# A gated delta rule in chunks of 128 tokens instead of 64, inside a two-layer float32 trunk

## The chip, the cores and the metric

The kernel runs on one core of a Trainium2 chip, as one program with one launch. The metric is the device time of the whole program in microseconds (us), less is better. Five engines work side by side, each through its own instructions in order: TensorE (PE; its weight loads are shown apart as PEld), VectorE (DVE), ScalarE (ACT), GpSimd (POOL) and SyncE (SP), which here only issues DMA transfers.

## The reference

Two layers over 1024 tokens of width 1024, all in float32. Layer 0 is softmax attention over a band of chunks and an MLP; layer 1 is a gated delta rule (8 heads of 128) and an MLP; every MLP is a squared ReLU of width 4096. The change touches the delta rule alone. Per head and per chunk of tokens the reference does this:

```python
gc = jnp.cumsum(g, axis=-1)                      # log decay within a chunk
decay = jnp.exp(jnp.where(incl, gc[..., :, None] - gc[..., None, :], -jnp.inf))
L = jnp.where(strict, jnp.einsum('bhnid,bhnjd->bhnij', kb, k) * decay, 0.0)
M = L + jnp.eye(CHUNK)
sol = lax.linalg.triangular_solve(M, rhs, lower=True, unit_diagonal=True)  # gives u and w
qk = jnp.einsum('bhnid,bhnjd->bhnij', q, k) * decay
def step(state, inp):                            # one chunk after the other
    v_new = u_c - w_c @ state
    o_c = qd_c @ state + qk_c @ v_new
    state = state * gl_c + kd_c.T @ v_new
```

CHUNK is 64 in the reference. The result of the recurrence does not depend on the chunk's length; a longer chunk means fewer steps of `step` and a larger triangular system.

## The kernel before

The program is one stream: attention, its output projection and MLP (lines 569 to 1640), the delta rule (`deltanet`, lines 1674 to 2582), then the second output projection and MLP. Activations are stored transposed, 128 features by 1024 tokens.

The delta rule's stage is planned while the program is written out. `dn_run` walks through 34 dense panels (w_in for k, q, v and z of 8 heads, then two panels of the output projection, named "o"), each of 128 output features; a panel is two halves of 24 matmuls of 128x512 (the two "o" panels here are one half each). After every dense matmul `turn()` lets each of some ten tasks emit a step if a cost table (`Clock`) says that its inputs are ready and its engines are not too far behind; tasks are asked in the order of `PRIORITY`. What comes out is a fixed order on each engine. So the small work of the delta rule stands between the dense matmuls on PE, and a wait of a small matmul holds up the dense matmuls behind it. Where the dense matmuls need something that is not there by the table, `idle()` moves the table's time on.

The tasks, all per head of 8 pairs of 64-token chunks (128 tokens a pair, index p):

- `dn_decays`: adds a mask to the log decays (POOL), takes exp (ACT, one instruction per pair), writes to DRAM the two 64x64 blocks on the diagonal of each 128x128 square.
- `dn_blocks`: k times k on PE, times the decays on DVE (tile U); writes U's 32x32 diagonal blocks (`ud`) and the 32x32 block beside them in each 64 (`u12`) to DRAM.
- `dn_solves`: inverts the 32x32 triangular blocks of four heads at once on DVE (tiles fz, ft, fu).
- `dn_inverse`: builds the inverse of each 64x64 triangle from the 32x32 ones: read `u12` back, scale by rk (POOL), 16 matmuls of 32x32 (`tp<-xa,ua`), scale on DVE, 16 more (`tp<-Zh,ua`), copy into Z on ACT.
- `dn_prep_keys`, `dn_prep_queries`, `dn_prep_values`: transposes, q times k with the decays read back (tile dc, scaled by rk on POOL), the products with Z that give u (tile vb) and w (half of tile WQ; the other half is q times its decay, written by POOL).
- `dn_scans(odd)`: the recurrence, one task for even heads and one for odd ones. Per chunk of 64: one matmul of the state st with 128 columns of WQ, which hold w of this chunk and the decayed q of the same chunk side by side (`s<-st,WQ`), then DVE forms vn, then `s<-vn,kd` and `s<-vn,qk` on PE, then DVE forms the next state st and ACT copies 64 rows of the output (o). kd and qk are full 128x128 operands, whose other half meets zeros in vn or qk.
- `dn_outs`, `dn_reload`: norm and gate of a head's output, transposes (`tp<-ident,o`), to DRAM and back as the two-part operands xs of the output projection.

Names of tiles in the trace leave buffer numbers out: s is both PSUM tiles of the scan (s1 and s2), tp the shared auxiliary PSUM bank (two buffers), acc the dense one. A float32 matmul of 128x128 leaves two records in the trace, a dense one (float32r) leaves one. Nearly all instructions of the stage have line 163, that of the helper which records them, so groups are told apart by tiles.

Of the kernel before, what the change touches and what calls it, by code (L numbers as in the profile page):

```python
# [7 lines left out]
F32 = mybir.dt.float32  # L8
# [199 lines left out]
class Trunk:  # L208
# [1465 lines left out]
    def deltanet(self, rhs, finish):  # L1674

        tc = self.tc
        with ExitStack() as es:
# [10 lines left out]
                "s1": Ring(2, lambda: self.sc.tile([P, P], F32, name=self.nm("s1"), tag="s1")),  # L1688
# [186 lines left out]
    def dn_gates(self):  # L1875
# [12 lines left out]
        self.u12 = self.dr.tile([8, 2, 32, 8, 32], F32, name="u12")  # L1888
        d1.tile([P, 16], F32, name="room3")
# [6 lines left out]
        self.vn = [[d1.tile([P, P], F32, name=f"vn{o}{e}") for e in range(2)] for o in range(2)]  # L1896
        for v in self.vn:
            for e in range(2):
                nc.gpsimd.memset(v[e][64 - 64 * e : 128 - 64 * e], 0.0)

        self.qks = [d1.tile([P, 8, P], F32, name=f"qk{n}") for n in range(2)]
        for qk in self.qks:
            for e in range(2):
                nc.gpsimd.memset(qk[64 * e : 64 * e + 64, :, 64 * e : 64 * e + 64], 0.0)
# [18 lines left out]
        nc.gpsimd.memset(mask[0:64, 64:128], -BIG)  # L1923
# [23 lines left out]
        for s in (1, 2, 4, 8, 16, 32):  # L1947
            va, vb = (t.rearrange("q (e t) -> q e t", e=2) for t in (g0, g1))
            nc.vector.tensor_copy(vb[:, :, :s], va[:, :, :s])
            nc.vector.tensor_tensor(vb[:, :, s:], va[:, :, s:], va[:, :, : 64 - s], ALU.add)  # L1950
            g0, g1 = g1, g0
        gc = g0
        gv = gc.rearrange("q (e t) -> q e t", e=2)
        eg, ed, bg, ng, nb = t64("eg"), t64("ed"), t64("bg"), t64("ng"), t64("nb")
        nc.scalar.activation(eg, gc, AF.Exp)
        nc.vector.tensor_tensor(
            ed.rearrange("q (e t) -> q e t", e=2), gv[:, :, 63:64].broadcast_to([NQ, 2, 64]), gv, ALU.subtract)
# [8 lines left out]
        for n, t in enumerate((gc, nb, eg)):  # L1966
# [62 lines left out]
    def dn_decays(self, odd):  # L2029
# [3 lines left out]
        for h in range(odd, 8, 2):  # L2033
# [127 lines left out]
    def dn_blocks(self):  # L2161

        nc, db = self.nc, self.db
        for h in range(8):
# [88 lines left out]
    def dn_inverse(self, h):  # L2253
# [3 lines left out]
        X = self.dq.tile([P, 8, 32], F32, name=self.nm("xa"), tag="xa")  # L2257
        U12 = self.dq.tile([P, 8, 32], F32, name=self.nm("ua"), tag="ua")
        for e in range(2):
# [11 lines left out]
        for b in range(4):  # L2271
# [3 lines left out]
            if b % 2 == 0:  # L2275
                nc.sync.dma_start(X[s], xd[r].rearrange("p c i -> c p i"))
# [23 lines left out]
        yield  # L2300
        for e in range(2):
            r, o = slice(64 * e, 64 * e + 32), slice(64 * e + 32, 64 * e + 64)
            nc.scalar.activation(Z[r, :, o], ps[r], AF.Copy)
        self.give("tp", tp)
# [50 lines left out]
    def dn_prep_queries(self):  # L2355
        nc, db = self.nc, self.db
        for h in range(8):
            yield from self.until("q", h)
            qT = self.heads.pop(("q", h))
            dc = self.dq.tile([P, HB], F32, name=self.nm("dc"), tag="dc").rearrange("p (q t) -> p q t", t=64)  # L2360
# [310 lines left out]
```

## Time and profile before

| | |
|---|---|
| runs | 2565.44, 2566.76, 2565.82 us; median 2565.82 |
| profiled execution | 2565.74 us, of which the span from first to last instruction is 2564.0 |
| PE, PEld busy | 96%, 80% of the span |
| DVE, ACT, POOL busy | 72%, 47%, 50% |
| mean granted TensorE clock | 0.990 |
| the delta rule's stage | from about 1199 us to 1838 us of the span |

A row of the chain or the timeline gives start and length in us, the engine, the line, the operation, and in brackets how long the engine was idle just before and what released it. Matmuls are pipelined, so what one costs is read from the distance between starts, not from the length of a record. A group's row (by line, operation and tile) has the count, the busy time in us and the mean of one in ns, then the idle time before its instructions. A row of a window gives its borders, its length, each engine's busy time, the granted clock, the DMA share and GB/s.

### The profile page before, as it was taken

How to read it: one execution, taken by the hardware profiler on the slowest of the kernel's cores; microseconds unless marked ns; L12 is line 12 of the kernel's file. 1: busy time of each engine (PE TensorE's matmuls, PEld its weight loads, DVE VectorE, ACT ScalarE, POOL GpSimd, SP SyncE). 2: the span in 40 equal slices, each digit the busy share in tenths (PEclk: the TensorE clock that was granted, in tenths of full speed). 3: DMA queues.
4: the chain of work that ended last, by engine and by line, in shares of the span. 5: the costliest groups of instructions: out<-in, count | busy, mean ns of one | idle time of the engine just before them, and what ended most of it. 6: DMA issues, size and time to landing. Idle time of an engine off the chain costs nothing.

```text
span 2564.0 us, 36694 instructions
## 1 busy us (share of the span) xinstructions
PE 2462.7 (96%) x12638; PEld 2055.4 (80%) x12638; DVE 1848.5 (72%) x3299; ACT 1206.2 (47%) x2267; POOL 1280.2 (50%) x1088
## 2 busy tenths in 40 slices
PE   8999999999999999998888899999999999999997
PEld 6888888787888888886677788888787888787886
DVE  6666656678776688877588867666678777688887
ACT  6666567535555433334674333333335555433323
POOL 2444455615666466565474333332313766466655
PEclk9999999999999999999999999999999999999998
DMA  4222224424555966743443212213323555977752
GB/s 159 71 64 72 74 78 126 151 83 160 208 208 217 350 236 231 262 148 110 117 141 112 69 59 68 70 62 103 121 99 140 208 203 209 334 244 255 247 172 82
DMA packets 193082, 392.43 MB, mean 153 GB/s; under 512 B 54960, under 2 KB 61552, under 8 KB 192896
## 3 DMA queue, kind: packets, MB, share of 16 engines
q1 hardware_dynamic: 176048, 355.46, 41.2%
q10 hardware_dynamic: 16848, 34.63, 3.6%
q8 instruction: 100, 1.64, 0.3%
q14 instruction: 86, 0.70, 0.1%
HBM read 254.06 MB, written 127.57 MB: 149 GB/s over the span
## 4 chain that ended last, share of the span: by engine, by line
PE 63%; DVE 10%; issue 3%; DMA 3%; ACT 1%; POOL 1%; SPq 0%; ACTq 0%; DVEq 0%; POOLq 0%
PE y L1013 25%; PE z L1013 12%; PE acc L163 8%; PE acc L1013 7%; PE tp L163 3%; PE s L163 3%; PE acc L279 2%; PE acc L278 2%; PE acc L277 2%; DVE fz L163 1%; DVE ft L163 1%; DVE x L1518 1%; DMA xs<-gt 1%; DMA wraw<-in_w_down_dram 0%; DVE xs L394 0%
## 5 line engine op out<-in xcount | busy, mean ns | idle before, releaser
L163 PE MATMUL acc<-xs,whi 128*128 128x512 f32 x1808 | 637.9, 414 | 8.9 <-DVE xp L163 4.1
L163 PEld LDWEIGHTS acc<-xs,whi 128*128 128x128 f32 x1808 | 332.7, 191 | 58.4 <-DVE xp L163 4.9
L163 PE MATMUL acc<-xs,wlo 128*128 128x512 f32 x896 | 367.4, 410 | 3.4 <-POOL wlo L163 3.4
L1013 PE MATMUL y<-xs,whi 128*128 128x512 f32 x1008 | 311.6, 390 | 5.2 <-DVE x L1518 1.8
L163 POOL TENSOR_TENSOR wlo<-wraw,whi 128x512 fp32r<-128x512 f32 x126 | 166.8, 1324 | 253.2 <-ACT whi L163 213.3
L1028 POOL TENSOR_TENSOR s<-wraw 128x256 f32<-128x256 f32 (+1 forms) x93 | 91.7, 987 | 351.1 <-DVE a L1019 171.5
L1019 DVE TENSOR_TENSOR wlo<-wraw,whi 128x512 fp32r<-128x512 f32 (+1 forms) x182 | 209.9, 1153 | 26.3 <-ACT whi L1022 26.3
L1013 PEld LDWEIGHTS y<-xs,whi 128*128 128x128 f32 x1008 | 188.9, 188 | 47.2 <-DVE x L1518 2.6
L1022 ACT ACTIVATE whi<-wraw 128x512 fp32r<-128x512 f32 (+2 forms) x191 | 146.5, 767 | 122.9 <-PE y L1013 87.0
L1013 PE MATMUL y<-xs,wlo 128*128 128x512 f32 x504 | 196.3, 390 | 0.0
L1022 ACT ACTIVATE a<-s 128x256 fp32r<-128x256 f32 x122 | 63.8, 525 | 281.4 <-PE y L1013 143.4
L1013 PE MATMUL y<-xs,a 128*128 128x512 f32 x732 | 187.9, 392 | 7.0 <-DVE x L1518 7.0
L163 PEld LDWEIGHTS acc<-xs,wlo 128*128 128x128 f32 x896 | 171.6, 192 | 28.6 <-POOL wlo L163 5.2
L1518 DVE TENSOR_TENSOR x<-y,x 128x512 f32<-128x512 f32 x240 | 165.1, 688 | 35.0 <-PE y L1013 28.4
L1013 PEld LDWEIGHTS y<-xs,a 128*128 128x128 f32 x732 | 136.0, 188 | 40.6 <-DVE x L1518 10.9
L1013 PE MATMUL y<-xs,ahi 128*128 128x512 f32 x512 | 158.6, 391 | 7.8 <-ACT nt L1207 7.8
L1013 PE MATMUL acc<-xs,whi 128*128 128x512 f32 x528 | 162.8, 390 | 0.0
L163 POOL TENSOR_SCALAR pr<-pr,rs 128x640 f32<-128x640 f32 (+4 forms) x128 | 88.6, 696 | 128.9 <-DVE rs L163 97.8
L1013 PE MATMUL z<-xs,whi 128*128 128x512 f32 x480 | 147.8, 389 | 0.0
L1095 DVE TENSOR_TENSOR c<-c 128x512 fp32r<-128x512 f32 x112 | 120.2, 1078 | 31.2 <-POOL c L1025 28.4
L163 POOL TENSOR_TENSOR cy<-cy,cz 128x512 f32<-128x512 f32 x48 | 64.3, 1340 | 147.9 <-DVE cz L163 121.2
L163 DVE CUSTOM_DVE_ANT_0 pr<-sp,bias 128x640 f32<-128x640 f32 (+4 forms) x128 | 83.8, 655 | 63.8 <-PE sp L163 62.8
(345 smaller groups left out, 6218.7 us busy)
## 6 DMA issues: line engine op xcount, KB each, us to landing
xs<-gt SPq DMA_DIRECT2D x256, 256.0 KB, 4.7
gt<-c SPq DMA_DIRECT2D x112, 512.0 KB, 2.8
wraw<-in_w_up_dram SPq DMA_DIRECT2D x64, 512.0 KB, 3.9
wraw<-in_w_down_dram SPq DMA_DIRECT2D x64, 512.0 KB, 4.4
r<-gr SPq DMA_DIRECT2D x88, 256.0 KB, 3.5
wraw<-in_w_in_dram SPq DMA_DIRECT2D x32, 512.0 KB, 3.5
gr<-ssum ACTq DMA_DIRECT2D x62, 256.0 KB, 3.1
wraw<-in_w_qkv_dram SPq DMA_DIRECT2D x30, 512.0 KB, 3.3
```

Of the source, the lines that this page charges most:

```text
L163: return call(*args, **more)
L277: nc.tensor.matmul(ps, hi[:, k], xh, start=(k == 0), stop=False)
L278: nc.tensor.matmul(ps, hi[:, k], xl, start=False, stop=False)
L279: nc.tensor.matmul(ps, lo[:, k], xh, start=False, stop=(k == KT - 1))
L1013: nc.tensor.matmul(ps, w[:, k], x, start=bool(first and f), stop=bool(last and e), skip_group_check=True)
L1019: self.nc.vector.tensor_tensor(lo, src, hi.bitcast(F32), ALU.subtract)
L1022: self.nc.scalar.activation(hi, src, AF.Copy)
L1028: self.nc.gpsimd.tensor_tensor(out, x, y, ALU.add)
L1095: nc.vector.tensor_tensor(t[z][:, HB:].bitcast(F32R), t[z][:, HB:], t[z][:, :HB], ALU.subtract)
L1518: nc.vector.tensor_tensor(x, ps, x, ALU.add)
```

## The change

- The scan takes 8 steps of 128 tokens per head instead of 16 of 64. A step has two matmuls with the state (w and decayed q, 128 columns each) instead of one, one with kd and one with qk; vn, o and st are full 128x128. The first step of a head has no state and takes u in place of vn, without a copy. The PSUM tile s1 doubles to hold both products.
- The decays keep the whole 128x128 squares: the mask loses its cross-chunk part, one contiguous 512 KB DMA per head replaces two strided ones of 128 KB, dc doubles to 128x1024, and its scaling on POOL with it; the product of q and k with dc becomes one 128x512 DVE instruction in place of two of 64x256.
- The inverse gets a level: the 64x64 blocks of U beside the diagonal go to DRAM and back (`u34`, tile U34, named ub in the trace), are scaled by rk on POOL (64x512); 8 more 32x32 matmuls (`ua,Zh`) give the transposed corner, which ACT copies into X; 8 matmuls of 64x64 (`X,ub`), a scaling on DVE, 8 more of 64x64 (`Zh,ub`), a copy on ACT. One more block of the 32x32 inverses is loaded into X per head.
- The cumulative sum of the log decays has a seventh doubling step; memsets of vn and qk go, one of X comes.

```diff
@@ dn_decays, dn_blocks
-            for e in range(2):
-                r = slice(64 * e, 64 * e + 64)
-                nc.sync.dma_start(self.decay[h, r], v[r, :, r])
+            nc.sync.dma_start(self.decay[h], v)
...
+            nc.sync.dma_start(self.u34[h], U[0:64, :, 64:128])
@@ dn_inverse
+        nc.sync.dma_start(U34[0:64], self.u34[h])
...
+        nc.gpsimd.tensor_tensor(U34[0:64], U34[0:64], wide(self.rk[0:64, h], 64, 64), ALU.mult)
...
-            if b % 2 == 0:
-                nc.sync.dma_start(X[s], xd[r].rearrange("p c i -> c p i"))
+            if b < 3:
+                nc.sync.dma_start(self.X[s, :, 32 * (b % 2) : 32 * (b % 2) + 32], xd[r].rearrange("p c i -> c p i"))
...
+        o = slice(32, 64)
+        for p in range(8):
+            nc.tensor.matmul(ps[o, p], Z[o, p, o], hT[o, p], start=True, stop=True, tile_position=(32, 32))
+        yield
+        nc.scalar.activation(self.X[o, :, 0:32], ps[o], AF.Copy)
...
+        r, o = slice(0, 64), slice(64, 128)
+        for p in range(8):
+            nc.tensor.matmul(ps[o, p], U34[r, p], self.X[r, p], start=True, stop=True, tile_position=(0, 64))
+        yield
+        nc.vector.tensor_tensor(U34[o], ps[o], wide(nbr[o], 64, 64), ALU.mult)
...
+        for p in range(8):
+            nc.tensor.matmul(ps[r, p], U34[o, p], Z[o, p, o], start=True, stop=True, tile_position=(64, 0))
+        yield
+        nc.scalar.activation(Z[r, :, o], ps[r], AF.Copy)
@@ dn_prep_queries
-            nc.gpsimd.tensor_tensor(dc, dc, wide(self.rk[:, h], P, 64), ALU.mult)
+            nc.gpsimd.tensor_tensor(dc, dc, wide(self.rk[:, h], P, P), ALU.mult)
...
-                for e in range(2):
-                    r = slice(64 * e, 64 * e + 64)
-                    nc.vector.tensor_tensor(qk[r, s, 64 - 64 * e : P - 64 * e], ps[r, :, r], dc[r, s], ALU.mult)
+                nc.vector.tensor_tensor(qk[:, s], ps, dc[:, s], ALU.mult)
@@ dn_scans
-            for c in range(16):
...
-                    nc.tensor.matmul(ps, wq, st, start=True, stop=False, skip_group_check=True)
-                    yield
-                    nc.vector.tensor_tensor(vn[r], u[r, p], ps[r], ALU.subtract)
+            for p in range(8):
+                vn = u[:, p]
...
+                    nc.tensor.matmul(ps[:, 0], WQ[:, p, 0], st, start=True, stop=True, skip_group_check=True)
+                    ready = self.clock.end
+                    nc.tensor.matmul(ps[:, 1], WQ[:, p, 1], st, start=True, stop=False, skip_group_check=True)
+                    self.clock.end = ready
+                    yield
+                    vn = db.tile([P, P], F32, name=self.nm("vn"), tag=f"vn{odd}")
+                    nc.vector.tensor_tensor(vn, u[:, p], ps[:, 0], ALU.subtract)
...
-                nc.scalar.activation(o[r, p], ps[x], AF.Copy)
+                nc.scalar.activation(o[:, p], ps[:, 1], AF.Copy)
```

Since the order on each engine is planned, the change also moves work that its text leaves alone. Three places follow.

PE, at the inverse of head 7, while heads 5 and 6 are scanned. Before (xa and ua are the two operands of the first 32x32 products, acc the dense panel's bank):

```order
L163 MATMUL tp_16653<-xa_16215,ua_16216 32x32 x16
L163 MATMUL acc_16566<-xs_11822,whi_16393 128x512
L163 MATMUL s_3508_16672<-vn_12244,kd_16341 128x128
L163 MATMUL s_3506_16651<-vn_12244,qk_12251 128x128
L163 MATMUL acc_16566<-xs_11822,wlo_16394 128x512
L163 MATMUL s_3509_16678<-vn_12243,kd_15831 128x128
L163 MATMUL s_3503_16645<-vn_12243,qk_12250 128x128
L163 MATMUL acc_16566<-xs_11824,whi_16393 128x512
L163 MATMUL tp_16688<-Zh_12240,ua_16216 32x32 x16
L163 MATMUL acc_16566<-xs_11824,whi_16393 128x512
```

Now, at the inverse of a head late in the stage:

```order
L163 MATMUL s_3367_16192<-st_16157,WQ_15952 128x128 x2
L163 MATMUL tp_16170<-ua_15720,Zh_12239 32x32 x8
L163 MATMUL acc_16165<-xs_11810,wlo_15969 128x512
L163 MATMUL acc_16165<-xs_11812,whi_15968 128x512 x2
L163 MATMUL acc_16165<-xs_11812,wlo_15969 128x512
L163 MATMUL acc_16165<-xs_11814,whi_15968 128x512 x2
L163 MATMUL s_3371_16222<-vn_16207,kd_15497 128x128
L163 MATMUL s_3367_16192<-vn_16207,qk_12245 128x128
L163 MATMUL acc_16165<-xs_11814,wlo_15969 128x512
L163 MATMUL acc_16165<-xs_11816,whi_15968 128x512 x2
L163 MATMUL acc_16165<-xs_11816,wlo_15969 128x512
L163 MATMUL tp_16235<-X,ub_15721 64x64 x8
```

Three groups of eight small matmuls come per head, each among dense ones, and a scan step shows two matmuls with WQ.

PE, the last steps of head 7's scan, at the end of the stage. Before (acc_17974 is the first "o" panel's bank):

```order
L163 MATMUL s_3822_18071<-st_18065,WQ_17577 128x128
L163 MATMUL s_3823_18074<-vn_12245,kd_17214 128x128
L163 MATMUL s_3822_18071<-vn_12245,qk_12251 128x128
L163 MATMUL s_3825_18080<-st_18077,WQ_17577 128x128
L163 MATMUL acc_17974<-xs_17925,whi_17827 128x512 x2
L163 MATMUL acc_17974<-xs_17925,wlo_17828 128x512
L163 MATMUL s_3827_18088<-vn_12244,kd_17214 128x128
L163 MATMUL s_3825_18080<-vn_12244,qk_12251 128x128
L163 MATMUL acc_17974<-xs_17926,whi_17827 128x512
L163 MATMUL s_3830_18099<-st_18093,WQ_17577 128x128
```

Now (acc_17742 is the second half of head 7's z panel, the last one ahead of the "o" panels):

```order
L163 MATMUL s_3679_17720<-vn_17710,kd_17092 128x128
L163 MATMUL s_3674_17704<-vn_17710,qk_12246 128x128
L163 MATMUL acc_17651<-xs_11822,whi_17491 128x512 x2
L163 MATMUL acc_17651<-xs_11822,wlo_17492 128x512
L163 MATMUL s_3681_17730<-st_17724,WQ_17448 128x128 x2
L163 MATMUL acc_17651<-xs_11824,whi_17491 128x512 x2
L163 MATMUL acc_17651<-xs_11824,wlo_17492 128x512
L163 MATMUL s_3681_17730<-vn_17734,qk_12246 128x128
L163 MATMUL acc_17742<-xs_11811,whi_17491 128x512 x2
```

Before, the scan's last steps stood within the first "o" panel, two of them with no dense matmul between; now the last scan matmul stands ahead of 72 dense ones: 24 of z and 48 of the two "o" panels.

POOL, around the scaling of dc for the second head. Before:

```order
L163 TENSOR_TENSOR ua_14025<-ua_14025,rk 32x256 x2
L163 TENSOR_TENSOR wlo_14011<-wraw_13717,whi_14010 128x512
L163 TENSOR_TENSOR cy_14020<-cy_14020,cz_14021 128x512
L163 TENSOR_TENSOR dc_13905<-dc_13905,rk 128x512
L163 TENSOR_TENSOR cy_14158<-cy_14158,cz_14159 128x512
```

Now:

```order
L163 TENSOR_TENSOR cy_13919<-cy_13919,cz_13920 128x512
L163 TENSOR_TENSOR ua_13923<-ua_13923,rk 32x256 x2
L163 TENSOR_TENSOR ub_13924<-ub_13924,rk 64x512
L163 TENSOR_TENSOR dc_13902<-dc_13902,rk 128x1024
L163 TENSOR_TENSOR wlo_14045<-wraw_13727,whi_14044 128x512
```

The new scaling of ub and the longer one of dc now follow one another on POOL.

More of the change, by code (lines that the diff above doesn't have):

```diff
@@ L1687, in deltanet @@
                 "tp": Ring(2, self.aux), "acc": Ring(2, self.bank), "nt": Ring(3, self.nt),
[L1688 removed]
+                "s1": Ring(2, lambda: self.sc.tile([P, 2, P], F32, name=self.nm("s1"), tag="s1")),
                 "s2": Ring(2, lambda: self.sc.tile([P, P], F32, name=self.nm("s2"), tag="s2"))}
@@ L1888, in dn_gates @@
         self.u12 = self.dr.tile([8, 2, 32, 8, 32], F32, name="u12")
+        self.u34 = self.dr.tile([8, 64, 8, 64], F32, name="u34")
         d1.tile([P, 16], F32, name="room3")
@@ L1894, in dn_gates @@
             self.Zh.append(z)
-        self.vn = [[d1.tile([P, P], F32, name=f"vn{o}{e}") for e in range(2)] for o in range(2)]
-        for v in self.vn:
-            for e in range(2):
-                nc.gpsimd.memset(v[e][64 - 64 * e : 128 - 64 * e], 0.0)
+        self.X = d1.tile([P, 8, 64], F32, name="X")
+        nc.gpsimd.memset(self.X[0:32, :, 32:64], 0.0)
         self.qks = [d1.tile([P, 8, P], F32, name=f"qk{n}") for n in range(2)]
-        for qk in self.qks:
-            for e in range(2):
-                nc.gpsimd.memset(qk[64 * e : 64 * e + 64, :, 64 * e : 64 * e + 64], 0.0)
         yield
@@ L2303, in dn_inverse @@
             nc.scalar.activation(Z[r, :, o], ps[r], AF.Copy)
+        self.give("tp", tp)
+        yield
+        tp = yield from self.take("tp")
+        ps = tp.rearrange("p (q t) -> p q t", t=64)
+        r, o = slice(0, 64), slice(64, 128)
[3 more added lines that the diff above has]
+        nc.vector.tensor_tensor(U34[o], ps[o], wide(nbr[o], 64, 64), ALU.mult)
+        self.give("tp", tp)
+        yield
+        tp = yield from self.take("tp")
+        ps = tp.rearrange("p (q t) -> p q t", t=64)
+        for p in range(8):
+            nc.tensor.matmul(ps[r, p], U34[o, p], Z[o, p, o], start=True, stop=True, tile_position=(64, 0))
+        yield
+        nc.scalar.activation(Z[r, :, o], ps[r], AF.Copy)
         self.give("tp", tp)
@@ L2359, in dn_prep_queries @@
             qT = self.heads.pop(("q", h))
-            dc = self.dq.tile([P, HB], F32, name=self.nm("dc"), tag="dc").rearrange("p (q t) -> p q t", t=64)
+            dc = self.whole("dc").rearrange("p (q t) -> p q t", t=P)
             nc.sync.dma_start(dc, self.decay[h])
@@ L2386, in dn_prep_queries @@
                 yield
-                for e in range(2):
-                    r = slice(64 * e, 64 * e + 64)
-                    nc.vector.tensor_tensor(qk[r, s, 64 - 64 * e : P - 64 * e], ps[r, :, r], dc[r, s], ALU.mult)
+                nc.vector.tensor_tensor(qk[:, s], ps, dc[:, s], ALU.mult)
                 self.give("tp", tp)
                 yield
-            WQ = db.tile([P, 8, 4, 64], F32, name=self.nm("WQ"), tag="WQ")
+            WQ = db.tile([P, 8, 2, P], F32, name=self.nm("WQ"), tag="WQ")
             nc.gpsimd.tensor_tensor(
-                WQ[:, :, 1:3], qT.rearrange("p (q e t) -> p q e t", e=2, t=64),
-                row.rearrange("p (q e t) -> p q e t", e=2, t=64), ALU.mult)
+                WQ[:, :, 1], qT.rearrange("p (q t) -> p q t", t=P), row.rearrange("p (q t) -> p q t", t=P), ALU.mult)
             self.heads["qq", h] = WQ, qk
@@ L2470, in dn_scans @@
                 ready = self.clock.end
-                nc.tensor.matmul(ps, qk[:, p], vn, start=st is None, stop=True, skip_group_check=True)
+                nc.tensor.matmul(ps[:, 1], qk[:, p], vn, start=st is None, stop=True, skip_group_check=True)
                 self.clock.end = ready
                 yield
-                if c < 15:
+                if p < 7:
                     nst = db.tile([P, P], F32, name=self.nm("st"), tag=f"st{odd}")
```

48 lines of the change are left out of this document (19 added, 29 removed).

## The prediction

> **What bounds the kernel now.** I read the engines' shares first, then the delta rule's stage alone (the change touches nothing else), then what a matmul costs there, and last what PE waits for.
>
> ```profile
> PE 2462.7 (96%) x12638; PEld 2055.4 (80%) x12638; DVE 1848.5 (72%) x3299; ACT 1206.2 (47%) x2267; POOL 1280.2 (50%) x1088
> ...
> 1405.00:1815.00 410.00, 392.36 (x2668) 339.77 (x2668) 275.80 (x703) 151.53 (x326) 131.56 (x100) 0.99 0.23 74
> 1805.00:1838.50 33.50, 28.78 (x134) 22.26 (x132) 22.51 (x58) 12.59 (x27) 8.90 (x7) 0.90 0.27 86
> ```
>
> PE is the bound: over the stretch in which heads are scanned (the first window row) it is busy for 392 of 410 us. So the stage's length is PE's work plus what PE stands still or runs at a lower clock; a change on another engine counts only through PE's waits. The last 33.5 us stand out: clock 0.90 and 4.7 us idle. Those waits, over the scanned stretch and the tail together, are these:
>
> ```profile
> PE s L163 <- DVE vn L163: 11.1, 11, 3.0
> PE s L163 <- DVE st L163: 4.9, 4, 2.7
> PE s L163 <- DVE ry L163: 4.3, 3, 2.0
> PE tp L163 <- DVE o L163: 1.1, 2, 0.9
> PE s L163 <- ACT o L163: 0.3, 1, 0.3
> ```
>
> All but one row are the scan's own hand-overs (s is its PSUM), 20.6 us in 19 waits.
>
> **Part 1, scan matmuls removed.** The groups by tile:
>
> ```profile
> L163 PE MATMUL s<-vn,qk 128*128 128x128 f32 x256 | 50.3, 279 | 0.0
> L163 PE MATMUL s<-vn,kd 128*128 128x128 f32 x240 | 48.2, 283 | 11.1 <-DVE vn L163 11.1
> L163 PE MATMUL s<-st,WQ 128*128 128x128 f32 x240 | 47.1, 281 | 9.5 <-DVE st L163 4.9 <-DVE ry L163 4.3 <-ACT o L163 0.3
> ```
>
> Two records make a matmul, so 128 + 120 + 120 = 368 matmuls now. After: 8 steps per head with 7 x 2 (WQ) + 7 (kd) + 8 (qk) = 29, times 8 heads 232. That is 136 fewer. The price from starts in the timeline, and from twelve dense matmuls in the chain:
>
> ```profile
> 1801.31 0.38 PE L163 MATMUL s<-vn,kd 128*128 128x128 f32 x2
> 1801.53 0.39 PE L163 MATMUL s<-vn,qk 128*128 128x128 f32 x2
> 1801.67 0.47 PE L163 MATMUL acc<-xs,whi 128*128 128x512 f32 x1
> 1801.98 0.39 PE L163 MATMUL acc<-xs,wlo 128*128 128x512 f32 x1
> ...
> 1379.67 2.73 PE acc L163 x12
> ```
>
> A dense one is 2.73/12 = 0.227; from 1801.31 to 1801.98 stand kd, qk and one dense, 0.67, so a scan matmul is (0.67 - 0.227)/2 = 0.222. 136 x 0.222 = **-30.2 us**.
>
> **Part 2, small matmuls added**: per head 8 of 32x32 and 16 of 64x64. Of the first there is a row, of the second none:
>
> ```profile
> 1671.04 0.48 PE L163 MATMUL acc<-xs,whi 128*128 128x512 f32 x1
> 1671.45 1.09 PE L163 MATMUL tp<-xa,ua 32*32 32x32 f32 x32
> 1672.47 0.50 PE L163 MATMUL acc<-xs,whi 128*128 128x512 f32 x1
> 1672.81 0.38 PE L163 MATMUL s<-vn,kd 128*128 128x128 f32 x2
> ```
>
> 32 records take 1.02 us, 0.032 each; the dense matmul ahead takes 0.41 instead of 0.227 and the one behind 0.34, so going to the small form and back costs 0.18 + 0.11 = 0.29. A group of 8 matmuls of 32x32 (16 records) is 0.51 + 0.29 = 0.80. For 64x64, between 0.032 a record and the 0.111 of a 128x128 one: 0.80 to 2.07 a group. I take the straight line in the number of columns, 0.058 a record, because the two known prices are near 32 and 128 parts of one slope: 0.93 + 0.29 = 1.22. Per head 0.80 + 2 x 1.22 = 3.24, times 8 **+25.9 us**; bounds 16.9 (cheap records, and the 32x32 group without a return of its own) and 39.5.
>
> The eight 64x64 matmuls of a group all load weights into the same rows of the array. The Trainium skill, TensorE: Matmul & The Clock Gate, section The mechanism (of its Part 3), says that a weight load overlaps a running matmul only if its row group differs; with its price for a load (columns over 1.2 GHz, 53 ns for 64) a record would be an estimated 0.11 us and this part about 39. The xa rows above speak against it: 16 records there share one row group, and at load plus stream they could not average 0.032.
>
> **Part 3, the end of the stage.**
>
> ```profile
> 1805.18 0.38 PE L163 MATMUL s<-st,WQ 128*128 128x128 f32 x2
> ...
> 1818.38 0.80 PE L163 MATMUL s<-vn,kd 128*128 128x128 f32 x2 [2.04 <-DVE vn L163]
> ...
> 1838.02 0.66 PE L163 MATMUL tp<-ident,o 128*128 128x128 f32 x4 [0.92 <-DVE o L163]
> 1838.44 0.48 PE L277 MATMUL acc<-xs,whi 128*128 128x512 f32 x1
> ```
>
> From the first of these rows to the last, the next block's start, are 33.3 us. PE's order has there 71 dense matmuls (16.1), 26 of the scan (5.8) and 8 transposes (two groups of four, 0.42 each by the last two rows): 22.7 us. So 10.6 us are lost: single steps of head 7 with little between them, and after the 2.04 us gap a clock that is down (0.90 over the window). After the change the last scan matmul has 72 dense ones behind it. What is late next is the reload: the first "o" panel reads head outputs that ACT and DVE or POOL split just ahead. By ACT's order 12 operations stand between the scan's last matmul and the sixth of those splits; at 0.62 each, held up by the last z half, and with a POOL half of 1.29, I estimate that they end 14.0 us after the scan, where PE needs them at 11.6:
>
> ```profile
> 1808.03 0.61 ACT L163 ACTIVATE xs<-cy 128x512 fp32r<-128x512 f32 x1
> 1808.73 1.29 POOL L163 TENSOR_TENSOR xs<-cy,xs 128x512 fp32r<-128x512 f32 x1 [7.79 <-ACT xs L163]
> ```
>
> 2.4 us stay lost of 10.6: **-8.2 us**; bounds -10.6 and 0.
>
> **Part 4, waits in the rest of the scan.** 20.6 less 3.4 in the tail leaves 17.3 us of waits. The clock falls after some of them, and not after others:
>
> ```profile
> 1432.00:1436.00 4.00, 2.75 (x8) 2.29 (x9) 3.86 (x9) 0.00 (x0) 1.18 (x2) 0.56 0.99 316
> 1436.00:1440.00 4.00, 4.00 (x18) 3.61 (x17) 3.25 (x9) 1.22 (x3) 0.58 (x1) 0.58 0.33 129
> 1460.00:1464.00 4.00, 2.83 (x39) 2.34 (x40) 3.65 (x12) 0.63 (x1) 0.00 (x0) 0.90 0.00 0
> 1464.00:1468.00 4.00, 4.00 (x43) 3.07 (x42) 1.31 (x5) 0.53 (x2) 0.00 (x0) 0.67 0.00 0
> 1652.00:1656.00 4.00, 3.79 (x24) 3.38 (x25) 3.52 (x16) 0.90 (x2) 0.84 (x1) 1.00 0.58 200
> ```
>
> 4 x (0.44 + 0.42) = 3.4 us behind a 2.69 us wait, 4 x (0.10 + 0.33) = 1.7 behind another, nothing behind the longest (2.97): 5.1 in all. Why the waits come:
>
> ```profile
> 1648.27 2.36 POOL L163 TENSOR_TENSOR WQ<-qT,row 128x1024 f32<-128x1024 f32 x1
> 1648.37 2.29 DVE L163 TENSOR_SCALAR ov<-ov 128x8 f32<-128x8 f32 x1
> ...
> 1651.45 0.17 DVE L163 TENSOR_SCALAR rt<-ov 128x8 int32<-128x8 int32 x1
> ...
> 1652.21 0.49 PE L163 MATMUL s<-vn,kd 128*128 128x128 f32 x2 [2.97 <-DVE vn L163]
> ...
> 1703.52 1.04 POOL L163 TENSOR_TENSOR dc<-dc,rk 128x512 f32<-128x512 f32 x1
> 1703.62 0.97 DVE L163 TENSOR_TENSOR ru<-ry 128x8 f32<-128x8 f32 x1
> ```
>
> A DVE instruction on 8 columns (0.17 otherwise) lasts as long as the POOL instruction beside it; the scan's DVE step queues behind it, and PE's next scan matmul, with all dense ones behind, waits. The Trainium skill, SBUF — State Buffer, section SBUF: two separate sides, calls it an exclusive lock on a port pair that DVE and GpSimd share, held for the whole instruction; the trace agrees (2.29 beside 2.36).
>
> So each long POOL instruction is a trap for a scan step that happens to fall on it. With 64 steps instead of 128 in the same time, half as many fall: 17.3 to 8.6, and 5.1 to 2.5. Against that, POOL holds grow:
>
> ```profile
> L163 POOL TENSOR_TENSOR o<-o,ov 128x1024 f32<-128x1024 f32 x7 | 13.3, 1899 | 25.8 <-DVE ov L163 24.8 <-DVE xp L163 1.0
> L163 POOL TENSOR_TENSOR ua<-ua,rk 32x256 f32<-32x256 f32 x16 | 10.9, 683 | 13.6 <-DVE st L163 10.5 <-DMA ua<-u 2.5
> L163 POOL TENSOR_TENSOR dc<-dc,rk 128x512 f32<-128x512 f32 x8 | 8.5, 1056 | 0.0
> ```
>
> dc goes from 1.06 to 1.90 (the 1024-wide row), ub adds one of 1.06 (512 wide): 8 x (0.84 + 1.06) = 15.2 us on the 131.6 that POOL is busy in the window, 12% more; 8.6 becomes 9.7. Sum: 9.7 - 17.3 + 2.5 - 5.1 = **-10.2 us**; bounds -22.4 (no wait left) and +15.2 (none saved, every added hold reaches PE).
>
> **Edits at nothing.** DVE sheds 72 instructions of vn, 64 of st and the split qk products, and gains eight 64x512 scalings; ACT sheds 64 copies of o and gains 16. Neither bounds a stretch; fewer of them is in Part 4 already, and if the new copies were not covered by the dense matmuls between the inverse's groups, they would cost a fraction of a us per head. SP issues 16 DMAs more among over a thousand; the decays go as one contiguous transfer where two strided ones went. The stage's first part (to 1405 us), where PE waits on masks, exps and conversions, keeps its instructions, so its waits stay; I allow 2 us either way. The memsets and the seventh doubling step stand beside dense matmuls.
>
> **Sum**: -30.2 + 25.9 - 8.2 - 10.2 = -22.7. The profiled execution took 2565.74 (span 2564.0 and 1.74 around it), 0.08 under the median of the runs shown. 2565.82 - 22.7 = **2543.1 us**.
>
> **The rivals.**
> - *64x64 groups at the price of 128x128.* 39.5 instead of 25.9: 2556.7. For it: no row of that form. Against it: records have been cheaper with fewer columns. The skill's row-group rule would give this result.
> - *No waits left in the scan.* Part 4 at -22.4: 2530.9. For it: DVE has less to do, and the steps have more time. Against it: the POOL holds stay and PE's order puts kd only three dense matmuls behind WQ, as before.
> - *The reload takes the scan's place at the end.* Part 3 at 0: 2551.3. For it: the "o" panel waits on one conversion after another. Against it: half of them can run while z's last half is multiplied.
> - *Slower: DVE is locked out longer.* POOL's order has ub and dc behind one another, and behind ua: over 4 us of holds per head (2 x 0.68 + 1.06 + 1.90) on the engine that every step needs twice. If no wait is saved, all 15.2 us reach PE and four of the new gaps lower the clock as the 2.69 us one did (3.4 each, 13.6), Part 4 is +28.8: 2582.1. It decides from waits of some 30 us in the scan (17.3 + 12.5, which would eat Parts 1 to 3). For it: DVE sits locked for the whole of the dc instruction today (0.97 beside 1.04). Against it: most holds today (100 POOL instructions in 410 us) cost PE nothing.
>
> **How the numbers follow.** Forecast 0.50; no waits 0.18; 64x64 dear 0.13; reload 0.12; slower 0.07. Differences under 0.2% (5 us) can't be told from no change here. Forecast, no waits and reload are faster, and so is part of the dear 64x64 (0.05): 0.85. The rest of that (0.08), where it meets a weaker Part 4, is no change; 0.07 is slower. The range takes in the forecast, reload, most of the dear case up to 2561, and the no-waits case down to 2527: about 0.84.
>
> **What would show it.** Part 1: 464 records on s instead of 736, starts still 0.22 apart. Part 2: distance from the first to behind the last of eight 64x64, 0.93 by my line, 1.78 by the rival. Part 3: no step of the scan after the last z half, the clock at 1.00 to the end, waits of acc on xs of 2 to 3 us in its place. Part 4: waits of s on DVE near 10 us. I am wrong if PE's waits on s stay near 20 us, or if dense matmuls around the 64x64 groups lose more than 0.3 us each time.

## The result, and the profile after

| | before | changed |
|---|---|---|
| median of four runs on one chip | 2566.29 us | 2552.03 us (2550.89 to 2553.20) |
| ratio, 95% interval | | 0.9945 [0.9928, 0.9962] |
| profiled execution, its span | 2565.74, 2564.0 | 2551.33, 2549.2 |
| the delta rule's stage, from its matmul at 1199 us to the next block's first | 639.4 | 627.9 |
| tail: to the next block's first matmul, from the row at 1805.18 before, from the last scan matmul now | 33.3 | 27.9 |

14.3 us less were measured, 22.7 were forecast. The engines' shares of the changed kernel, then the stretch in which heads are scanned and the tail as windows (busy time of PE, PEld, DVE, ACT, POOL, then the granted clock):

```profile
PE 2455.1 (96%) x12750; PEld 2045.8 (80%) x12750; DVE 1810.2 (71%) x3157; ACT 1194.7 (47%) x2219; POOL 1287.6 (51%) x1088
```

```profile
1405.00:1795.00 390.00, 379.71 (x2794) 325.74 (x2793) 241.52 (x567) 141.11 (x280) 143.05 (x108) 0.99 0.25 80
1799.00:1827.50 28.50, 22.97 (x86) 16.80 (x85) 19.33 (x44) 11.88 (x22) 12.06 (x9) 0.82 0.43 133
```

PE is still the bound. The tail has become shorter, and yet its clock is lower than before (0.82, was 0.90): it has lost its scan work, not its idle time. What PE waits for, from the scanned stretch to the end of the tail:

```profile
PE s L163 <- DVE st L163: 3.9, 2, 3.3
PE s L163 <- DVE ry L163: 2.9, 2, 1.9
PE tp L163 <- DVE o L163: 2.5, 1, 2.5
PE tp L163 <- issue: 2.5, 2, 2.1
PE acc L163 <- ACT xs L163: 1.4, 2, 1.1
...
PE s L163 <- DVE vn L163: 0.2, 1, 0.2
```

The waits of s fell from 20.6 us in 19 to 7.0 us in 5. The others are new, but for 1.1 us on o and 0.2 on xs: those on o and xs lie in the tail (5.5 us together with the shorter ones on xs), those named "issue" and another of 0.8 us are the inverse's matmuls and the key transposes (3.3 us). The groups of the changed kernel show the scan's records (224 + 112 + 96, and 16 + 16 in the first steps that read u from vb, 464 in all, as counted) and what POOL now does:

```profile
L163 PE MATMUL s<-st,WQ 128*128 128x128 f32 x224 | 34.2, 275 | 6.8 <-DVE st L163 3.9 <-DVE ry L163 2.9
L163 PE MATMUL s<-vn,qk 128*128 128x128 f32 x112 | 21.9, 277 | 0.0
L163 PE MATMUL s<-vn,kd 128*128 128x128 f32 x96 | 18.8, 278 | 0.2 <-DVE vn L163 0.2
L163 POOL TENSOR_TENSOR dc<-dc,rk 128x1024 f32<-128x1024 f32 x8 | 15.2, 1896 | 0.0
L163 POOL TENSOR_TENSOR ub<-ub,rk 64x512 f32<-64x512 f32 x8 | 8.7, 1087 | 4.0 <-PE s L163 3.5
```

### The profile page after: what moved, and what is told of

It is laid out like the page before. It is cut to its first block, busy times and chain, and to the rows that moved or that the text cites. A ratio compares the mean times of both kernels' runs of the same rounds, so it can differ in the third digit from the quotient of the medians.

```text
span 2549.2 us, 36712 instructions
## 1 busy us (share of the span) xinstructions
PE 2455.1 (96%) x12750; PEld 2045.8 (80%) x12750; DVE 1810.2 (71%) x3157; ACT 1194.7 (47%) x2219; POOL 1287.6 (51%) x1088
## 4 chain that ended last, share of the span: by engine, by line
PE 65%; DVE 8%; DMA 3%; issue 2%; ACT 1%; POOL 1%; SPq 1%; ACTq 0%; DVEq 0%; POOLq 0%
PE y L1013 25%; PE z L1013 12%; PE acc L163 10%; PE acc L1013 7%; PE tp L163 5%; PE s L163 2%; PE acc L279 2%; PE acc L278 2%; PE acc L277 2%; DVE ft L163 1%; DVE x L1518 1%; DVE fz L163 1%; DMA row<-grows 1%; DVE xs L394 0%; DMA xs<-gt 0%
```

## The experiments

All are compared with the kernel before on the same chip. Before's median was between 2565.85 and 2567.12 there; single runs of a kernel lie up to 6 us under its median and up to 11 above it, so that differences under about 4 us are read from the profiles, not from the times.

| run | what | median us | ratio, interval |
|---|---|---|---|
| | the change | 2552.03 | 0.9945 [0.9928, 0.9962] |
| e1 | 64x64 matmuls issued twice | 2569.24 | 1.0016 [1.0006, 1.0026] |
| e2 | 136 scan matmuls put back | 2581.90 | 1.0060 [1.0047, 1.0073] |
| e3 | head 7's second norm after the "o" panels | 2549.88 | 0.9934 [0.9919, 0.9949] |
| e4 | reload's low parts on DVE | 2547.09 | 0.9930 [0.9917, 0.9944] |
| e6 | e3 + e4 | 2552.68 | 0.9949 [0.9932, 0.9966] |
| e7 | e3, and the z halves reordered | 2552.82 | 0.9954 [0.9938, 0.9970] |
| e5 | dc and ub scaled on ACT | 2541.90 | 0.9903 [0.9888, 0.9918] |
| e8 | e5 + e3 + e4 | 2541.18 | 0.9904 [0.9890, 0.9918] |
| e9 | the kernel before, dc scaled on ACT | 2561.75 | 0.9984 [0.9974, 0.9994] |
| e10 | e5 + e4 | 2538.95 | 0.9893 [0.9880, 0.9907] |
| e11 | e5, and q's decay product on DVE | 2535.98 | 0.9882 [0.9867, 0.9897] |
| e12 | e11 + e4 | 2533.80 | 0.9870 [0.9854, 0.9887] |

### The two prices: e1 and e2

e1, at both 64x64 groups (the added loop does not enter the planner's table, so that nothing else moves):

```diff
         for p in range(8):
             nc.tensor.matmul(ps[r, p], U34[o, p], Z[o, p, o], start=True, stop=True, tile_position=(64, 0))
+        for p in range(8):
+            nc.tensor.real.matmul(ps[r, p], U34[o, p], Z[o, p, o], start=True, stop=True, tile_position=(64, 0))
```

> The changed kernel with its two groups of eight 64x64 matmuls per head issued twice (128 matmuls more in all, the same products into the same PSUM, so the output is the same; the order of everything else is kept). Theory (Part 2 costs what its records take, because PE bounds the stage): a group starts its records 0.067 us apart in the changed kernel (1633.06 to 1634.13 for 16), so 128 x 2 x 0.067 = +17.2 us on 2552.0: 2569. Rival A (the 64x64 groups stand in time that PE would wait anyway): +0 to +5, 2552 to 2557. Rival B (weight loads do not overlap, as records of 128x128 have it, 0.111 each): +28.4, 2580. Either way the second half of each group shows by its start distances what a 64x64 record costs when no change of form lies beside it.

Measured: 2569.24, +17.2. PE's timeline shows the two halves of one group and the dense matmul behind:

```profile
1654.56 1.14 PE L163 MATMUL tp<-Zh,ub 64*64 64x64 f32 x16
1655.54 1.09 PE L2320 MATMUL tp<-Zh,ub 64*64 64x64 f32 x16
1656.56 0.50 PE L163 MATMUL acc<-xs,wlo 128*128 128x512 f32 x1
```

From its first start to the dense matmul behind, the doubled group takes 2.00 us. A single one takes 1.07 in the changed kernel:

```profile
1633.06 1.14 PE L163 MATMUL tp<-X,ub 64*64 64x64 f32 x16
1634.13 0.50 PE L163 MATMUL acc<-xs,whi 128*128 128x512 f32 x1
```

So 16 records more cost 0.93 us, 0.058 each, a little over half of the 0.111 of a 128x128 one, and nothing hides them. For all 256 that is 14.9 us. The theory's 17.2 was reckoned with 0.067, the mean over a group whose start costs extra; that the median meets it to the digit is luck, since the 2.3 us between lie in the scatter. Rival A falls, and so does Rival B (0.111 a record): all sixteen load into the same rows. The Trainium skill, TensorE: Matmul & The Clock Gate, section The mechanism, says that a weight load overlaps a running matmul only if its row group differs. The trace does not agree: 0.058 us a record, where the prediction estimated 0.11 by that rule.

e2, in each step that has a state:

```diff
+                    for _ in range(2 + (p < 4)):
+                        nc.tensor.real.matmul(ps[:, 1], WQ[:, p, 1], st, start=True, stop=False, skip_group_check=True)
                     nc.tensor.matmul(ps[:, 1], WQ[:, p, 1], st, start=True, stop=False, skip_group_check=True)
```

> The changed kernel with 136 scan matmuls put back: the product of the decayed q with the state is issued three times (four times in steps 1 to 3 of a head) instead of once, into the same PSUM, so 368 scan matmuls are issued as before the change, still in 8 steps per head; the output is the same, and everything else keeps its order. Theory (Part 1: the gain is matmuls that PE no longer does, 0.222 each): +30.2 us, 2582, slower than the kernel before, and the waits of s stay near 7 us. Rival (the gain came from having half as many steps, and the matmuls themselves filled time in which PE waited): +10 us or less, 2562.

Measured: 2581.90, +29.9, with 5.3 us of waits of s from 1405 to 1790. Part 1 is settled: with the steps left at 8, 136 scan matmuls cost 0.22 us each, and the rival (10 us or less) falls. The waits of s stay low as well, so it is not the number of scan matmuls that makes them. The run also shows the rest of the change bare: with as many scan matmuls as before, it is 15.6 us slower than before.

### The tail: e3, e4, e6, e7

PE's waits in the changed kernel's tail, from its last scan matmul to the next block:

```profile
1799.21 0.38 PE L163 MATMUL s<-vn,qk 128*128 128x128 f32 x2
...
1809.70 0.50 PE L163 MATMUL acc<-xs,whi 128*128 128x512 f32 x1 [1.11 <-ACT xs L163]
1811.06 0.79 PE L163 MATMUL acc<-xs,whi 128*128 128x512 f32 x1 [0.85 <-POOL xs L163]
1813.24 0.80 PE L163 MATMUL acc<-xs,whi 128*128 128x512 f32 x1 [0.54 <-DVE xs L163]
1817.00 1.09 PE L163 MATMUL tp<-ident,o 128*128 128x128 f32 x4 [2.53 <-DVE o L163]
1827.08 0.39 PE L277 MATMUL acc<-xs,whi 128*128 128x512 f32 x1
```

27.87 us for 72 dense matmuls and 8 transposes (16.3 + 0.8): 10.7 us lost, as much as before the change (10.6). The longest wait is not the reload's. It is the transposes of head 7's second half, which PE's order has inside the first "o" panel, and for which DVE has to do a norm first. In the full timeline DVE's steps of that norm stand beside POOL's splits:

```profile
1811.29 1.28 POOL L163 TENSOR_TENSOR xs<-cz,xs 128x512 fp32r<-128x512 f32 x1 [0.28 <-ACT xs L163]
1811.39 1.21 DVE L163 TENSOR_SCALAR ov<-ov 128x4 f32<-128x4 f32 x1
...
1813.12 1.23 DVE L163 TENSOR_SCALAR rt<-ov 128x4 int32<-128x4 int32 x1
...
1816.16 0.69 DVE L163 TENSOR_TENSOR o<-o,ov 128x512 f32<-128x512 f32 x1
```

Two instructions on 4 columns take 1.21 and 1.23 us, the first as long as POOL's split beside it. PE is idle for much of 8 us, and its clock halves:

```profile
1812.00:1816.00 4.00, 1.93 (x4) 0.50 (x2) 3.69 (x12) 0.26 (x1) 2.32 (x2) 0.50 0.75 222
1816.00:1820.00 4.00, 3.00 (x9) 2.38 (x10) 2.60 (x5) 1.09 (x3) 0.00 (x0) 0.50 0.20 59
```

e3 moves that norm, e4 takes POOL out:

```diff
@@ e3: dn_outs, dn_run
                 yield from self.until("scan", h)
+                yield from self.until("panels")
                 yield from self.dn_out(h, 1, 2)
...
+        self.mark("panels")
         self.finish_tasks()
@@ e4: dn_reload
-                self.low(lo, t[:, :HB], hi, n % 2)
+                self.low(lo, t[:, :HB], hi)
```

> The changed kernel with the norm and the transposes of the second half of head 7's output put behind the two 'o' panels, where they stood inside the first of them on PE; DVE and ACT do the norm later too, behind the reload's splits. Theory (Part 3's gain was lost because these transposes wait for DVE's norm, 2.53 us, and the clock falls to 0.50 behind that gap): the gap goes and about 3 of the 5 us lost to the clock, less what waits for the reload's splits in its place: -3 to -5 us, 2547 to 2549. Rival (the splits of the reload on ACT, DVE and POOL are late by themselves, whatever the norm does): within 1 us of 2552, with acc on xs waiting 2 us more in the place of the 2.53.

> The changed kernel with the reload's low parts all on DVE (0.69 us each) instead of every second one on POOL (1.28 us each, 1.79 where DVE runs beside it). Theory (POOL instructions hold DVE's small norm steps, 1.21 and 1.23 us for 0.16 us instructions, and so the transposes that the 'o' panel waits for): these two go back to 0.16, the wait of PE on o falls from 2.53 by about 2 us and the wait on POOL's xs (0.85) goes, against three to four low parts of 0.69 more in DVE's queue: -1 to -3 us, 2549 to 2551. Rival (DVE is simply the longer queue there): +1 to +2 us, 2553 to 2554, with the wait on o as long as before.

Measured: 2549.88 and 2547.09, and tails of 23.15 and 23.46 us. Both theories (2547 to 2549, 2549 to 2551) miss by 1 to 2 us, e3's to the worse and e4's to the better side. In e3 the 2.53 us gap and the 0.54 ahead of it are gone, those on ACT's and POOL's splits stay (1.11 and 0.86), and 0.46 for the norm comes at the end. In e4, where the transposes at 1815.67 wait for nothing, the norm's steps are back at their own length. The tails as windows, e3's first, follow:

```profile
1811.69 0.17 DVE L163 TENSOR_SCALAR ov<-ov 128x4 f32<-128x4 f32 x1
1811.89 0.17 DVE L163 TENSOR_SCALAR rt<-ov 128x4 int32<-128x4 int32 x1
```

```profile
1797.81:1820.96 23.15, 20.22 (x84) 15.43 (x83) 18.57 (x40) 10.40 (x19) 11.05 (x8) 0.93 0.36 114
1798.39:1821.85 23.46, 19.22 (x84) 14.09 (x83) 19.49 (x49) 11.77 (x22) 2.91 (x2) 1.00 0.48 156
```

So both reasons are real: the norm stands in PE's way, and POOL holds it up. In e4 PE is still idle for 4.2 us (5.5 in the changed kernel), but in shorter pieces, 1.3 us at most, and the clock stays at 1.00; most of its gain is the clock. The tail gains 4.4 to 4.7 us in either profile; in the times, only e4's 4.9 us are near what can be told from nothing.

e6 has both edits. e7 has e3's, and runs the last two z panels as first half, first half, second half, second half, so that the reload may start one half panel earlier (core of the diff):

```diff
+            if n == len(jobs) - 4:
+                kept = c, h, hi, lo
+                self.zhalf(hi, lo, c, h, 0)
+                continue
+            if n == len(jobs) - 3:
+                self.zhalf(hi, lo, c, h, 0)
+                self.add(G["drl"], self.dn_reload())
+                self.zhalf(kept[2], kept[3], kept[0], kept[1], 1)
+                self.add(G["dw"], self.weights_marked(n + 1))
+                self.zhalf(hi, lo, c, h, 1)
+                continue
```

> Both edits of the end together: head 7's second norm and transposes behind the 'o' panels, and all low parts of the reload on DVE. By the profiles the tail (last scan matmul to the next block's first) took 27.9 us in the changed kernel, 23.2 with the first edit, 23.5 with the second, against 17.1 without any loss. Theory (two causes: PE waits for the norm, and POOL holds the reload's steps): together 19 to 21 us, -7 to -9 in the tail, 2543 to 2545. Rival (both edits free the same DVE steps, so the second adds nothing): 22.5 to 23.5 us, 2547 to 2548.

> The changed kernel with the last two z panels run as first half, first half, second half, second half, so that the reload, which overwrites the first half's operands, can start 24 dense matmuls (5.5 us) earlier; head 7's second norm and transposes stand behind the 'o' panels as before in the run that moved them. Theory (Part 3's term was right in its kind, and the reload is late because it may start only with the last half panel): the waits of acc on xs (3.0 us in the changed kernel) fall under 1 us, the tail to 18 to 20 us, -8 to -10: 2542 to 2544. Rival (ACT, DVE and POOL are taken up by other work there, the norm of head 6 and 7 and the weights of the 'o' panels, so an earlier start doesn't end earlier): as with the norm moved alone, 23 us, 2547 to 2549.

Measured: 2552.68 and 2552.82; no gain, and both theories miss on the time. e6's tail is 20.63 us as its theory said, but the transposes that were put off are no longer in it, and stop the next block at 1836.13 (the first row below). What follows the tail takes 728.6 us there and 722.1 in the changed kernel, which is nearly all that the tail gained; but that stretch takes 723 to 727 us in the other experiments, so that no run shows how much of it is the stop. The profiled execution is also the slowest of e6's six: at the 577th large dense matmul (128x128 weights) of the stage it is 8 us behind the changed kernel's (1417.2 against 1409.2), where nothing was edited, with the clock at 0.90 up to there instead of 0.95. e7's tail is 26.15 us: the reload's first split starts 6.9 us ahead of the last scan matmul instead of 1.5 behind it, but the later splits meet the weights of the "o" panels on POOL (wlo) and the norm of head 7's first half on DVE:

```profile
1836.13 0.63 PE L163 MATMUL tp<-ident,o 128*128 128x128 f32 x4 [2.67 <-DVE o L163]
```

```profile
1810.04 1.29 POOL L163 TENSOR_TENSOR wlo<-wraw,whi 128x512 fp32r<-128x512 f32 x1 [0.65 <-ACT whi L163]
1810.09 1.26 DVE L163 SCALAR_TENSOR_TENSOR ov<-ov,ry 128x4 f32<-128x4 f32 x1
...
1815.63 0.63 PE L163 MATMUL tp<-ident,o 128*128 128x128 f32 x4 [2.29 <-DVE o L163]
```

The rival's cause is what e7's rows show; its numbers (23 us, 2547 to 2549) were too low.

### POOL's rows of instructions: e5, e9, e11

In the changed kernel, the new 2.15 us wait of PE, and one of 1.92 us on the scan's state, have this in front of them:

```profile
1407.29 1.04 POOL L163 TENSOR_TENSOR ub<-ub,rk 64x512 f32<-64x512 f32 x1
1407.40 4.08 DVE L163 TENSOR_TENSOR fz<-fz,ft 128x60 f32<-128x60 f32 x1
1408.29 1.89 POOL L163 TENSOR_TENSOR dc<-dc,rk 128x1024 f32<-128x1024 f32 x1
1410.15 1.26 POOL L163 TENSOR_TENSOR wlo<-wraw,whi 128x512 fp32r<-128x512 f32 x1
...
1415.68 0.50 PE L163 MATMUL tp<-Zh,ua 32*32 32x32 f32 x11 [2.15 <-issue]
...
1533.89 1.03 POOL L163 TENSOR_TENSOR ub<-ub,rk 64x512 f32<-64x512 f32 x1
1534.06 2.75 DVE L163 TENSOR_SCALAR rt<-lv 128x8 int32<-128x8 int32 x1
1534.89 1.89 POOL L163 TENSOR_TENSOR dc<-dc,rk 128x1024 f32<-128x1024 f32 x1
...
1538.03 0.68 PE L163 MATMUL s<-st,WQ 128*128 128x128 f32 x4 [1.92 <-DVE ry L163]
```

The DVE instruction ends not with the POOL instruction beside it but with the last of POOL's row: 1407.40 + 4.08 = 1411.48 against 1410.15 + 1.26 = 1411.41, and 1536.81 against 1536.78. e5 takes dc and ub out of the rows; the planner's table still books them on POOL, so that the order of all else stays:

```diff
-        nc.gpsimd.tensor_tensor(U34[0:64], U34[0:64], wide(self.rk[0:64, h], 64, 64), ALU.mult)
+        self.clock.spend("gpsimd", "tensor_tensor", (U34[0:64], U34[0:64]), {})
+        for p in range(8):
+            nc.scalar.real.activation(U34[0:64, p], U34[0:64, p], AF.Copy, scale=self.rk[0:64, h, p : p + 1])
...
-            nc.gpsimd.tensor_tensor(dc, dc, wide(self.rk[:, h], P, P), ALU.mult)
+            self.clock.spend("gpsimd", "tensor_tensor", (dc, dc), {})
+            for p in range(8):
+                nc.scalar.real.activation(dc[:, p], dc[:, p], AF.Copy, scale=self.rk[:, h, p : p + 1])
```

> The changed kernel with the scalings of dc (128x1024) and of ub (64x512) by rk taken from POOL and put on ACT, as 8 instructions per head with a column each; the planned order of everything else is kept. The three longest waits of the scan that are left in the changed kernel (3.26 us at 1441, 1.92 at 1538, 1.00 at 1650) all stand behind a DVE instruction that lasted as long as a row of POOL instructions with ub or dc in it. Theory (Part 4: POOL's holds of DVE make the scan's waits): the two later ones go, the first shrinks by the 1.1 us of ub, and the clock behind it falls less: waits of s from 7.0 to about 3, time -3 to -5 us, 2547 to 2549. Rival (the scan waits because DVE's queue is long, and POOL is beside the point): waits of s stay near 7, and ACT's 16 instructions more per head (some 3.5 us) hold up its copies of o and its conversions: 0 to +4 us, 2552 to 2556.

Measured: 2541.90, twice the gain that the theory gave. All waits of the scan and of the auxiliary matmuls left from 1405 to 1790 are those below. The same instruction on 60 columns takes 0.22 us (second fence, from the timeline) instead of 4.08, and the wait at 1415.68 is gone with it; that one the theory had not counted.

```profile
PE s L163 <- DVE st L163: 2.6, 2, 2.0
PE tp L163 <- DVE kd L163: 0.7, 1, 0.7
PE s L163 <- DVE vn L163: 0.2, 1, 0.2
```

```profile
1406.73 0.22 DVE L163 TENSOR_TENSOR fz<-fz,ft 128x60 f32<-128x60 f32 x1
```

The last scan matmul moves from 1799.21 to 1790.96 (-8.3), of which the waits give 6.8 (10.3 to 3.5). The profiled execution is the slowest of e5's four and shows 6.2 us less in all, so that some 3 of the 10.1 us of the medians are placed by no row. The tail is the same to the hundredth (27.87). ACT's 128 new instructions (35.6 us) cost nothing that the trace shows.

e9 does the same to the kernel before, which has only dc, at 128x512:

> The kernel before, with its own scaling of dc (128x512) taken from POOL and put on ACT as 8 instructions of 128x64 per head; the order of everything else is kept. Theory (dc's place in POOL's rows of instructions costs either kernel; the change made it dearer, since ub and a doubled dc lengthen the rows): 1.06 us per head go instead of 2.93, so less than the 10 us that the same edit saved in the changed kernel: waits of s from 20.6 to 13 to 16, -4 to -7 us, 2559 to 2562, and the distance between chunk lengths grows from 14 to about 18 us once neither has the scaling on POOL. Rival (the scaling is dear only in the changed kernel, where ub stands ahead of it): within 1.5 us of 2566.

Measured: 2561.75, -4.1; the waits of s from 1405 to 1790 go from 17.3 (8.5 + 4.5 + 4.3) to 13.3:

```profile
PE s L163 <- DVE vn L163: 6.9, 7, 2.9
PE s L163 <- DVE st L163: 3.7, 3, 2.7
PE s L163 <- DVE ry L163: 2.7, 3, 2.0
```

The time is as expected; the waits are a little above it (17.1 us with the tail, as the 20.6 were counted, where 13 to 16 were expected). With neither kernel's dc and ub scaled on POOL, the 128-token chunks are worth 2561.75 - 2541.90 = 19.9 us instead of 14.3. e11 takes one more member out, the 2.42 us product of q with its decay, onto DVE (where it takes 1.3):

```diff
-            nc.gpsimd.tensor_tensor(
+            self.clock.spend("gpsimd", "tensor_tensor", (WQ[:, :, 1], row), {})
+            nc.vector.real.tensor_tensor(
                 WQ[:, :, 1], qT.rearrange("p (q t) -> p q t", t=P), row.rearrange("p (q t) -> p q t", t=P), ALU.mult)
```

> The changed kernel with the scalings of dc and ub on ACT, and also the product of q with its decay row (128x1024, 2.42 us on POOL, the last member of the row behind which the scan's longest wait, 2.01 us, is left) on DVE; the planned order is kept. Theory (POOL's rows hold DVE): that wait goes, 8 holds of 2.4 us turn into 8 DVE instructions of about 1.2: waits of s from 2.8 under 2, -1 to -3 us, 2539 to 2541. Rival (1.2 us in DVE's own queue ahead of a scan step costs as much as the hold did): 2541 to 2544, with waits of s as long.

Measured: 2535.98, 5.9 under e5 and 3 better than the theory's best; the intervals overlap a little. The last scan matmul comes 7.9 us earlier, at 1783.1; 3.0 of that is there already at the 577th dense matmul. The scan's waits add up to 0.8 us, and the clock is 1.00 over the scanned stretch:

```profile
PE s L163 <- DVE st L163: 0.6, 1, 0.6
PE s L163 <- DVE vn L163: 0.2, 1, 0.2
```

```profile
1405.00:1790.00 385.00, 383.49 (x2826) 329.48 (x2825) 237.09 (x584) 169.65 (x389) 106.02 (x86) 1.00 0.26 86
```

### Together: e8, e10, e12

> The changed kernel with the two edits of the end (norm and transposes later, low parts on DVE) and the scalings of dc and ub on ACT. Theory (the causes are apart in place, so the gains add): the sum of the two runs before, -7 to -9 and -3 to -5: -10 to -14, 2538 to 2542. Rival (the ACT scalings cost what they free): as the two edits of the end alone, 2543 to 2548.

> The changed kernel with the scalings of dc and ub on ACT and the reload's low parts on DVE, head 7's second norm left where it is. Theory (the tail's gain of 4.4 us, seen with the low parts alone, is kept where the next block doesn't wait for a norm that was put off): 2541.9 - 4.4, 2536 to 2539. Rival (whatever the tail gains, the next block waits for, as it did with both edits of the end): 2540 to 2543.

> The changed kernel with the three edits that paid: dc and ub scaled on ACT, the product of q with its decay row on DVE, the reload's low parts on DVE. Theory (the places are apart, the tail's edit is worth 3 us as it was beside the ACT scalings): 2536.0 - 3.0, 2531 to 2535, ratio to the kernel before about 0.987, with waits of s under 1 us and a tail near 23.5 us. Rival (the tail's gain is lost again in the next block): 2535 to 2538.

Measured: 2541.18, 2538.95 and 2533.80. The scan's gains add; the tail's hardly do. e8 lies in its theory's range (2538 to 2542), but not for the theory's reason: e5 alone gave all of it, and the edits of the end next to nothing. Its tail took 22.25 us (27.87 in e5), but what follows it 727.1 us, against 724.2 in e5. e10 and e12 are 3.0 and 2.2 us under the kernels without the tail's edit, which the intervals don't separate; both lie in their theories' ranges, but e12's tail is 25.3 us, not near 23.5. e12 beats both kernels: 0.987 of the kernel before, and 18 us under the change as it stood.

## Why the prediction was right, point by point

The direction was right, and 2552.03 lies in the range; 8.4 us of the forecast gain were missing. By the profiles the mechanisms of Parts 1, 2 and 4 held, and Part 3 (8.2 us) gained nothing.

- **Part 1, -30.2.** Right: e2 puts back 29.9.
- **Part 2, +25.9.** A little low. In the changed kernel's timeline a 64x64 group takes 1.07 (1633.06 to 1634.13), and the dense matmuls ahead (from 1632.74) and behind 0.09 and 0.11 more than 0.227: 1.27 for 1.22. A group of 32x32 takes 0.62, with the same 0.09 + 0.11: 0.82 for 0.80. 8 x (0.82 + 2 x 1.27) = 26.9. The straight line between the two known prices held (0.058 a record by e1, as taken); a group's start costs 0.14 more than its records, and the 0.18 that the prediction put on the matmul ahead is 0.09 where that one follows another dense matmul. The doubled price did not come.
- **Part 3, -8.2.** This step failed: the tail lost 10.7 us where 2.4 were foreseen. Its sum for the reload came out. The sixth split was set at 14.0 us behind the scan, and the last wait on a split ends at 1813.24, 14.0 us behind 1799.21 (that both say 14.0 is partly luck: this split ran on DVE, right behind the norm's step of 1.21 us); the waits on xs add up to 3.0, "2 to 3" were named. What it left out is that of the 8 transposes, which it counted as 0.84 us of work, four wait for a norm that starts only after the scan and runs beside POOL's splits; and the clock, which lost 5.1 us (0.82 over the tail) behind the idle time of all of them. "The clock at 1.00 to the end" was wrong. The rival "the reload takes the scan's place at the end" gave 2551.3, the nearest of all. That its total is met within 1 us is luck, since other terms moved too; its price of this step was right and its cause only half: e3 and e4 show the norm and POOL's hold on it beside the reload.
- **Part 4, -10.2.** Nearly right in sum. Waits of s outside the tail went from 17.3 to 7.0 (9.7 foreseen); of the clock 5.1 to 3.4 (2.5 foreseen), all behind the 3.26 us wait at 1441; against that came 3.3 us of waits elsewhere on PE: -10.3 - 1.7 + 3.3 = -8.7. What was foreseen of the holds themselves was too mild: the estimate priced the added POOL time as 12% more of the same, but ub and dc in one row make one long hold out of several. By e5, taking both out is worth 10 us. That half as many steps fall on the holds fits the fall of the waits; no run varied the number of steps alone.
- **Slower: DVE is locked out longer.** The mechanism is real, and e9 shows that it costs the kernel before 4 us too; with 7.0 us of waits it stayed far from the point at which it decides (some 30).
- **No waits left in the scan.** It was not this kernel, but e11 comes near its number (2536.0, 2530.9 given) by taking the holds away.
- **Edits at nothing.** They hold for ACT (e5 loads it with 128 instructions more, unseen) and for the queues, in that no wait of PE in the scanned stretch or the tail is put down to a DMA. The stage's first part was given 2 us either way. The 577th large dense matmul (the first of the 13th panel) comes at 1409.2 instead of 1403.0. Of these 6 us the waits make 1.4 (27.8 against 26.4) and the clock 1.7 (0.95 against 0.96); the rest is other small work, since PE's order up to there isn't the same. In the five experiments that leave that part alone (e2, e3, e4, e6, e7) its waits are 25.1 to 26.9 us and its clock 0.90 to 0.94, so that the 3.1 us can't be told from scatter.

The measured terms add up to -30.2 + 26.9 + 0 - 8.7 = -12.0, and the stage became 11.5 us shorter. With the first part's 3.1 that leaves some 3 us that PE gained and that I can't place. The last 3.4 us of the span's 14.8 came behind the stage (725.6 to 722.1 us from the next block's start), where nothing was changed; in the twelve experiments' profiles that stretch takes 723 to 729 us, and I read them as scatter.

## What to carry to other kernels

When a chain of waits is taken away from a stretch, list everything else there that waits for another engine, work that was counted by its length alone too: the four transposes were 0.4 us of work and 2.5 us of waiting. An engine that is half idle can still hold up another one: look at the longest instances of a short instruction, not at its mean, and at what stood beside them. A gain at the end of a stage counts only once the next stage's start has been looked at.

## What the runs showed of the hardware that was not expected

- **Holds add up over a row.** An instruction of DVE was held through two POOL instructions (2.75 us) and three (4.08 us), which by their rows followed each other without a gap, and ended with the last. The Trainium skill, SBUF — State Buffer, section SBUF: two separate sides, says that the lock lasts for the whole instruction; the trace agrees for one, and adds that DVE did not get in between two of them. The instruction of the 4.08 us took 0.22 without the row.
- **Small matmuls in one row group.** Sixteen records of 64x64 more in a group, all loading into the same 64 rows, took 0.058 us each; the 32 of 32x32 in a row of the kernel before took 0.032 each (1.02 us), and 128x128 ones take 0.111. Over these three forms the price goes with the columns. The start of a group of 64x64 adds 0.14 us.
- **The clock does not follow the waits one by one.** After the changed kernel's 3.26 us wait it was 0.81, 0.50 and 0.84 in the next three windows of 4 us; in e5 a wait of 2.01 us at the same place was followed by 0.70, 0.50 and 0.95, the same 3.4 us lost. After the 1.92 us wait at 1538 there is no such window. In the stage's first part, where PE waited for 25 to 28 us in all six, it was 0.95 in the changed kernel and 0.90 to 0.94 in the five experiments that leave that part alone.
